# Router threshold and first expert pair: copies on VectorE, the p product's stores on GpSimd's queue and from other buffers, the first pair's columns gathered one 128 at a time

## The chip, the cores and the metric

One core of one Trainium2 chip. The metric is the device time of the kernel in microseconds (us). The kernel before took 1686.97 us, the median of 3 runs (1686.44 to 1687.9).

## The reference, cut to what matters

Two transformer blocks run one after the other on 512 tokens of width 1024, all in float32. The first block ends in an expert-choice mixture: 16 experts, and each takes its 64 best tokens.

```
logits = einsum('btd,de->bte', h, w_router)
affinity = softmax(logits, axis=-1)                       # 512 tokens x 16 experts
gate, idx = lax.top_k(swapaxes(affinity, 1, 2), 64)
xe = h[idx]                                               # 64 tokens of each expert
a = einsum('becd,edf->becf', xe, w_gate)
u = einsum('becd,edf->becf', xe, w_up)
ye = einsum('becf,efd->becd', silu(a) * u, w_down) * gate
out.at[idx].add(ye)                                       # back to the tokens
```

The second block needs, near its end, `p_2 @ w_ple_2` (512x256 by 256x1024). It depends on inputs alone.

## The kernel before

The order of the work on each engine is written by hand: an instruction goes into its engine's queue in the order of the source, and each engine works its queue from the front. SP issues the weight loads, ACT and GpSimd (POOL) a few other DMAs.

**Output projection and router (up to L1226).** `out_quarter` runs the last product of the first block's attention part in four quarters on PE. Beside it `half_T`, `half_mm`, `rms`, `logit` and `soft` compute the router's softmax, one 128-token tile `t` after the other. `rms(t)` adds two sums on VectorE (DVE), scales them there (L186), takes the power on POOL (L182), and issues the store of the tile's rows to `x1_d` in DRAM from ACT (L1114). `x1_d` is read again much later, by the indirect gathers (L1323) of pairs 1 to 7.

**The p product (L1156 to L1169).** `pw_tile(i)` computes one half of one token tile of `p_2 @ w_ple_2`: two matmuls on PE, a copy of the PSUM bank by ACT (L1166), and after the second half of a tile a store to `pw_d` in DRAM, issued by ACT (L1168). There are eight such halves. Tiles 0 and 3 are copied to `xe[:, 0]`, tile 1 to `xe[:, 1]`, tile 2 to a part of `pk`. They are spread over the router so that PE has work: halves 0 and 1 beside the softmax of the last tile, 2 to 5 beside the top-64 search, 6 and 7 beside the threshold's use. `pw_d` is read back near the end of the kernel.

**Top 64 (L1229 to L1258).** The affinities are transposed (L1220) to 64 rows of 128, and DVE takes the 64 largest of each row in eight rounds (L1236, L1238) into `tops`. Then four sorted lists per expert are merged: two of them are moved to other partitions (L1244 by DVE, L1245 by ACT), a first maximum is taken (L1246), and twelve small DVE instructions sort and merge down to the threshold `thr`. All of it lies in the buffers `affT` and `tops`, two of the four buffers of the pool `tp`; the others of the pool serve `xT`, then `Gu` and `Gs`.

**Slots (L1260 to L1294).** PE brings the threshold to all partitions (`rt`), DVE compares (L1263, L1264), PE counts (L1269 to L1273), and DVE builds one-hot matrices (`onehot`, L1287) of which token sits in which slot: `Gu[0]` for the first pair of experts, `Gs`, the same times the token's norm, and `Gu[1]`.

**Expert pairs (L1427 to L1513).** Two experts at a time, in eight pairs; each pair has three products: `pa_` (gate), `pu` (up), `py` (down). `pair_gemm` runs a product in four quarters; a quarter reads two weight tiles of 1 MB (`ew`), and right after a quarter's matmuls SP gets the loads that reuse those two buffers (`eload`). Loads for pair 0 are issued long before; further ones wait until a buffer comes free. For pair 0 the tokens' columns come from matmuls with `Gs`: `gather(k0, n)` writes `n` columns of 128 into one PSUM bank (8 PE instructions a column), and ACT copies each to `xe[:, 0, k]` (L1304). Quarter `q` needs columns 2q and 2q+1. Before, columns 0 to 3 are gathered ahead of quarter 0, columns 4 and 5 ahead of quarter 1, 6 and 7 ahead of quarter 2. The other pairs get their tokens by an indirect DMA on POOL's queue.

**Second block.** After the last pair the rest of the kernel runs mostly on PE.

Of the kernel before, what the change touches and what calls it, by code (L numbers as in the profile page):

```python
# [12 lines left out]
AF = mybir.ActivationFunctionType  # L13
# [5 lines left out]
NT = T // 128  # L19
# [44 lines left out]
def tile_two_blocks(ctx: ExitStack, tc: tile.TileContext, a, out):  # L64
    nc = tc.nc
    ACT, DVE, PE, POOL, SP = nc.scalar, nc.vector, nc.tensor, nc.gpsimd, nc.sync
# [33 lines left out]
    def bank(name="pb", shape=(512,), dt=F32):  # L100
        return cur["ps"].tile([128] + list(shape), dt, name=name, tag="b")
# [30 lines left out]
    for gi, g in enumerate(groups):  # L132
        r = 0
        for n in g:
            v, k = rows(n)
# [48 lines left out]
    def rstd(dst, src, n, eps):  # L184

        DVE.tensor_scalar(dst, src, 1.0 / n, eps, op0=OP.mult, op1=OP.add)  # L186
        power(dst)
# [130 lines left out]
    def run(gen):  # L318
        for _ in gen:
            pass  # L320
# [53 lines left out]
    p_ = bank()  # L374
# [667 lines left out]
    def xrow(t, s=slice(None)):  # L1042
        return xr[t // 2][:, t % 2, s]

    def half(n):
        return slice(n * 512, n * 512 + 512)

    def dcol(k):

        return slice(256 * (k // 2) + k % 2, 256 * (k // 2) + 256, 2)  # L1050

    ga2 = cp.tile([128, 8], F32, name="ga2")
    DVE.tensor_scalar(ga2, modd[:, 8:16], 1.0, None, op0=OP.add)
    DVE.tensor_mul(ga2, ga2, bmp[:, 16:24])
    sh2 = modd[:, 0:8]
# [16 lines left out]
    def s1(t):  # L1072
        return aff[:, t, 17:18]
# [4 lines left out]
    affT = tp.tile([128, 512], F32, name="affT", tag="t")  # L1078
    tops = tp.tile([128, 512], F32, name="tops", tag="t")
# [31 lines left out]
    def rms(t):  # L1111
        DVE.tensor_add(s1(t), sq1[:, t, 0:1], sq1[:, t, 1:2])
        rstd(s1(t), s1(t), D, 1e-6)
        ACT.dma_start(out=x1_d[t * 128:t * 128 + 128], in_=xrow(t))  # L1114

    pls, mxs = {}, {}
# [8 lines left out]
    def logit(t):  # L1125

        l = lg[:, t]
        DVE.tensor_add(l, l, pls[t])
        DVE.scalar_tensor_tensor(l, l, s1(t), rb, op0=OP.mult, op1=OP.add)
        mxs[t] = mx = small("mx", 2)  # L1130
        DVE.tensor_reduce(mx[:, 0:1], l, axis=mybir.AxisListType.X, op=OP.min)
        ACT.activation(l, l, AF.Exp, bias=mx[:, 0:1], scale=-1.0, accum_out=mx[:, 1:2])

    def soft(t):
        sm = mxs[t][:, 1:2]
        DVE.reciprocal(sm, sm)
        DVE.tensor_scalar(aff[:, t, :16], lg[:, t], sm, None, op0=OP.mult)


    pw_d = dp.tile([128, NT, D], F32, name="pw_d")  # L1140
    pw = {}
# [15 lines left out]
    def pw_tile(i):  # L1157
        t, n = i // 2, i % 2
        p_ = bank("pw")
        for k in range(2):  # L1160
            PE.matmul(p_, pw["p"][:, 1, k * 512 + t * 128:k * 512 + t * 128 + 128], pw["w"][:, k, half(n)],
                      start=(k == 0), stop=(k == 1))
            yield
        o = pw["p"][:, 0] if t == 2 else xe[:, t % 2].rearrange("p k c -> p (k c)") if t < 2 else \
            xe[:, 0].rearrange("p k c -> p (k c)")
        ACT.activation(o[:, half(n)], p_, AF.Copy)  # L1166
        if n:
            ACT.dma_start(out=pw_d[:, t], in_=o)  # L1168
        yield  # L1169


# [32 lines left out]
    xe = big("xe", [2, KT, 128])  # L1204
    half_mm(2, 1)
    half_T(NT - 1, 1)
    rms(2)
    logit(2)
    gpw = pw_tile(0)
    next(gpw)  # L1210
    soft(2)
    half_mm(NT - 1, 1)
    rms(NT - 1)
    logit(NT - 1)
    run(gpw)
    gpw = pw_tile(1)
    next(gpw)
# [24 lines left out]

    l0, l1, ls, lb = (affT[:, c:c + 64] for c in (129, 193, 257, 322))
    DVE.tensor_copy(ls[0:32], tops[32:64, 0:64])  # L1244
    ACT.activation(ls[64:96], tops[96:128, 0:64], AF.Copy)  # L1245
    DVE.tensor_tensor(l0[0:96], tops[0:96, 0:64], ls[0:96, ::-1], op=OP.max)  # L1246
    x_, y_, d = l0, l1, 32
    while d:
# [3 lines left out]
        x_, y_, d = y_, x_, d // 2  # L1252
# [3 lines left out]
    DVE.tensor_tensor(affT[:16, 0:65], affT[:16, 128:193], affT[:16, 321:386][:, ::-1], op=OP.min)  # L1256
    thr = cp.tile([16, 1], F32, name="thr")
    DVE.tensor_reduce(thr, affT[:16, 0:65], axis=mybir.AxisListType.X, op=OP.max)  # L1258

    rt = bank3("rt")  # L1260
    PE.transpose(rt[:, 0, 0:16], thr.to_broadcast([16, 128]), ident[:16, :16])
    th = rt[:, 0, None, 0:16].to_broadcast([128, NT, 16])
    DVE.tensor_tensor(ge[:, :, 0:16], aff[:, :, 0:16], th, op=OP.is_gt)  # L1263
    DVE.tensor_tensor(ge[:, :, 16:32], aff[:, :, 0:16], th, op=OP.is_equal)  # L1264
    gpw = pw_tile(6)
    next(gpw)

    cnt = rt[:, 1, 0:128].rearrange("p (t c) -> p t c", t=NT)
    PE.matmul(cnt, tri, ge, start=True, stop=False)  # L1269
# [2 lines left out]
    for t in range(NT):  # L1272
        PE.matmul(cnt[:, :, 16:32], ones, ge[:, t, None, 0:16].to_broadcast([128, NT, 16]), start=False,  # L1273
                  stop=(t == NT - 1))
# [17 lines left out]
    Gs = tmp("Gs", (NT, 128))  # L1292
    DVE.tensor_mul(Gs, Gu[0], aff[:, :, 17:18].to_broadcast([128, NT, 128]))
    onehot(1)  # L1294

    def gather(k0, n):

        p_ = bank("pg", (n, 128))
        for d in range(n):
            for t in range(NT):  # L1300
                PE.matmul(p_[:, d], xrow(t, dcol(k0 + d)), Gs[:, t], start=(t == 0), stop=(t == NT - 1))
        for d in range(n):
            k = k0 + d
            ACT.activation(xe[:, 0, k], p_[:, d], AF.Identity, bias=sh2[:, k:k + 1], scale=ga2[:, k:k + 1])  # L1304

    gt_ = cp.tile([128, 8], F32, name="gt_")
    sl = cp.tile([128, 8], F32, name="sl")
# [121 lines left out]
    for p in range(8):  # L1429
# [5 lines left out]
        pa_ = bank3("pa_")  # L1435
        side = []
        if p == 0:
            gather(0, 2)
            side = [lambda q=q: gather(2 * q, 2) for q in (1, 2, 3)]
        else:  # L1440
            side = [lambda: None] + [lambda t=t: combine(p - 1, t) for t in ((0,), (1,), (2, 3))]
        pair_gemm(pa_, i0, xlhs, side)
# [4 lines left out]
        side = [lambda: gates(p + 1) if p < 7 else None, lambda: gates(0) if not p else None]  # L1447
# [4 lines left out]
        for n in range(2):  # L1452
            p_ = bank("pg", (4, 128))
# [9 lines left out]
        side = []  # L1463
        if p < 7:
            slots(p + 1, 0)
            side = [lambda: None, lambda: slots(p + 1, 1)]
# [27 lines left out]
        for n in range(2):  # L1494
            for q, (k0, nk) in enumerate(lasts[n]):
# [8 lines left out]
                for k in range(k0, k0 + nk):  # L1504
                    for e in range(2):
                        PE.matmul(py[n][64 * e:64 * e + 64], hlhs(k, e), tiles[e][k - k0], start=(k == 0),  # L1506
                                  stop=(k == KT - 1), tile_position=(0, 64 * e))
# [480 lines left out]
```

## Time and profile before

| What | us |
|---|---|
| median of 3 runs | 1686.97 |
| profiled execution | 1687.58 |
| its span in the profile | 1685.8 |
| TensorE busy | 1624.6 (96% of the span) |
| VectorE busy | 924.6 (55%) |
| ScalarE busy | 568.6 (34%) |
| GpSimd busy | 58.1 (3%) |

The profiled execution is 0.61 us above the median, and 1.78 us of it lie outside the span. Times in the trace are counted from the start of the span. A matmul in float32 shows as two PE instructions; PE's matmuls overlap, so an instruction's duration is longer than the distance to the next.

### The profile page before, as it was taken

How to read it: one execution, taken by the hardware profiler on the slowest of the kernel's cores; microseconds unless marked ns; L12 is line 12 of the kernel's file. 1: busy time of each engine (PE TensorE's matmuls, PEld its weight loads, DVE VectorE, ACT ScalarE, POOL GpSimd, SP SyncE). 2: the span in 40 equal slices, each digit the busy share in tenths (PEclk: the TensorE clock that was granted, in tenths of full speed). 3: DMA queues.
4: the chain of work that ended last, by engine and by line, in shares of the span. 5: the costliest groups of instructions: out<-in, count | busy, mean ns of one | idle time of the engine just before them, and what ended most of it. 6: DMA issues, size and time to landing. Idle time of an engine off the chain costs nothing.

```text
span 1685.8 us, 20663 instructions
## 1 busy us (share of the span) xinstructions
PE 1624.6 (96%) x8266; PEld 1140.7 (68%) x8266; DVE 924.6 (55%) x1760; ACT 568.6 (34%) x1070; POOL 58.1 (3%) x69
## 2 busy tenths in 40 slices
PE   8999999999999996999999898999999999999997
PEld 5987787767888883433334333358898888877886
DVE  4667676565554342122321231168889999845555
ACT  5454544455323231110000001052436532354234
POOL 2000000000000000000000000010001000000000
PEclk9999999999999998999999999999999999999999
DMA  9232323111554595999999999963323233333341
GB/s 356 71 103 98 102 99 101 51 51 51 200 193 132 226 362 225 394 425 427 426 427 426 427 426 427 420 215 89 95 81 96 84 92 100 100 100 100 100 150 50
DMA packets 139396, 341.26 MB, mean 202 GB/s; under 512 B 6719, under 2 KB 91492, under 8 KB 115620
## 3 DMA queue, kind: packets, MB, share of 16 engines
q1 hardware_dynamic: 135504, 328.50, 52.0%
q0 software_dynamic: 2272, 6.58, 1.1%
q10 hardware_dynamic: 1524, 4.86, 0.8%
q8 instruction: 65, 1.06, 0.3%
q14 instruction: 31, 0.25, 0.0%
HBM read 333.62 MB, written 6.29 MB: 202 GB/s over the span
## 4 chain that ended last, share of the span: by engine, by line
PE 35%; DMA 11%; DVE 2%; issue 1%; ACT 1%; POOL 0%; POOLq 0%; SPq 0%; ACTq 0%; DVEq 0%
PE pb L297 9%; PE pb L298 9%; PE pb L299 9%; DMA ew<-w_exp_up 4%; DMA ew<-w_exp_down 4%; DMA ew<-w_exp_gate 3%; PE py L1358 1%; PE pv L299 1%; PE pv L297 1%; PE pv L298 1%; PE pa__6628 L1358 1%; PE pu L1358 1%; PE py L1506 1%; PE pb L1620 1%; DMA xe<-x_d,ix 1%
## 5 line engine op out<-in xcount | busy, mean ns | idle before, releaser
L256 DVE TENSOR_TENSOR wl<-wr,wh 128x512 fp32r<-128x512 f32 x340 | 229.5, 696 | 120.2 <-ACT wh L258 120.2
L258 ACT ACTIVATE wh<-wr 128x512 fp32r<-128x512 f32 x340 | 194.6, 621 | 111.3 <-PE pb L298 58.8
L1699 DVE SCALAR_TENSOR_TENSOR co<-cin,cols,co 128x512 f32<-128x512 f32 x240 | 191.4, 797 | 4.2
L297 PE MATMUL pb<-h2h,wh 128*128 128x512 f32 x432 | 170.7, 395 | 0.0
L298 PE MATMUL pb<-h2l,wh 128*128 128x512 f32 x432 | 168.3, 390 | 0.0
L299 PE MATMUL pb<-h2h,wl 128*128 128x512 f32 x432 | 168.3, 390 | 0.0
L297 PE MATMUL pb<-hxh,wh 128*128 128x512 f32 x320 | 130.4, 408 | 0.0
L1358 PE MATMUL pu<-ew,xe 128*64 128x512 f32 x512 | 116.3, 595 | 9.9 <-DMA ew<-w_exp_up 9.8
L298 PE MATMUL pb<-hxl,wh 128*128 128x512 f32 x320 | 125.2, 391 | 0.0
L299 PE MATMUL pb<-hxh,wl 128*128 128x512 f32 x320 | 125.1, 391 | 0.0
L1358 PE MATMUL py<-ew,hb 128*64 128x512 f32 x440 | 102.4, 596 | 2.7 <-DMA ew<-w_exp_down 2.7
L297 PEld LDWEIGHTS pb<-h2h,wh 128*128 128x128 f32 x432 | 81.1, 188 | 19.0 <-issue 2.4
L1358 PEld LDWEIGHTS pu<-ew,xe 128*64 128x64 f32 x512 | 38.7, 137 | 80.6 <-issue 60.9
L299 PEld LDWEIGHTS pb<-h2h,wl 128*128 128x128 f32 x432 | 81.1, 188 | 17.1
L298 PEld LDWEIGHTS pb<-h2l,wh 128*128 128x128 f32 x432 | 81.1, 188 | 16.9 <-issue 0.5
L1375 DVE TENSOR_TENSOR xr<-pg,xr 128x512 f32<-128x512 f32 x64 | 41.6, 686 | 69.2 <-PE pg L1374 67.9
L855 ACT ACTIVATE P<-P,m 128x512 f32<-128x512 f32 (+1 forms) x64 | 49.7, 777 | 85.8 <-DVE m L854 83.2
L1450 DVE TENSOR_TENSOR hb<-pu,hb 128x512 f32<-128x512 f32 x16 | 10.3, 686 | 122.8 <-PE pu L1358 63.7
L851 DVE CUSTOM_DVE_ANT_0 P<-s,cst,sink 128x512 f32<-128x512 f32 (+1 forms) x64 | 52.2, 815 | 46.3 <-PE s L848 45.9
L1358 PEld LDWEIGHTS py<-ew,hb 128*64 128x64 f32 x440 | 32.2, 137 | 61.7 <-issue 53.3
L299 PEld LDWEIGHTS pb<-hxh,wl 128*128 128x128 f32 x320 | 60.1, 188 | 13.6
L297 PEld LDWEIGHTS pb<-hxh,wh 128*128 128x128 f32 x320 | 60.2, 188 | 11.4 <-issue 2.3
(473 smaller groups left out, 3003.6 us busy)
## 6 DMA issues: line engine op xcount, KB each, us to landing
ew<-w_exp_gate SPq DMA_DIRECT2D x64, 1024.0 KB, 19.5
ew<-w_exp_up SPq DMA_DIRECT2D x64, 1024.0 KB, 19.7
wr<-w_in SPq DMA_DIRECT2D x58, 1024.0 KB, 5.9
ew<-w_exp_down SPq DMA_DIRECT2D x55, 1024.0 KB, 19.7
wr<-w_mod SPq DMA_DIRECT2D x16, 1024.0 KB, 5.1
wm<-w_mod SPq DMA_DIRECT2D x8, 1024.0 KB, 13.2
wr<-w_out SPq DMA_DIRECT2D x8, 1024.0 KB, 5.9
ew<-w_exp_down SPq DMA_DIRECT2D x16, 512.0 KB, 10.5
```

The costliest lines, as they stand in the source:

```text
L256: (lo_engine or DVE).tensor_tensor(lo[:, ks], raw[:, ks], hi[:, ks].bitcast(F32), op=OP.subtract)
L258: ACT.activation(hi[:, ks], raw[:, ks], AF.Copy)
L297: PE.matmul(ps, ah, bh, start=first, stop=False)
L298: PE.matmul(ps, ah, bl, start=False, stop=False)
L299: PE.matmul(ps, al, bh, start=False, stop=last)
L851: DVE.tensor_tensor_reduce(p_[:, :n], s2[:, self.s0:self.s0 + n], self.mask, 1.0, sink8[:, 4 * g + i:4 * g + i + 1], op0=OP.add, op1=OP.ma ...
L855: ACT.activation(p_[:, :n], p_[:, :n], AF.Exp, bias=m4[:, i:i + 1], scale=0.125, accum_out=sm[:, i:i + 1])
L1358: PE.matmul(ps[64 * e:64 * e + 64, n], lhs(k, e), tiles[e][kk][:, n * 512:n * 512 + 512], start=(k == 0), stop=(k == KT - 1), tile_positio ...
L1375: DVE.tensor_add(xrow(t, half(n)), p_, xrow(t, half(n)))
L1506: PE.matmul(py[n][64 * e:64 * e + 64], hlhs(k, e), tiles[e][k - k0], start=(k == 0), stop=(k == KT - 1), tile_position=(0, 64 * e))
L1620: PE.matmul(ps[m], w_[:, k, m * 128:m * 128 + 128], x_(k), start=(k == 0 and z == 0), stop=(k == KT - 1 and z == 2))
L1699: DVE.scalar_tensor_tensor(co[ct], cin[ct][:, k:k + 512], ctap(k, ct), co[ct], op0=OP.mult, op1=OP.add)
```

## The change

- The second list copy (L1245) moves from ACT to DVE.
- `pw_tile`: the stores to `pw_d` are issued by POOL. Tile 3 no longer goes to `xe[:, 0]`: its first half is copied to `affT`, its second to `tops`, and each half is stored by itself, so there are five stores in place of four.
- The first matmul of half 6 is issued ahead of the threshold's transposition, in place of behind the compares.
- `rms` of the last token tile is issued ahead of `soft(2)`; its store to `x1_d` is issued behind `logit` of that tile.
- `gather` takes a PSUM bank for each column, and ACT copies it before the next column's matmuls are issued. Columns 0, 1, 2 come ahead of quarter 0, then 3, 4, then 5, 6, then 7.

```diff
     def rms(t):
         DVE.tensor_add(s1(t), sq1[:, t, 0:1], sq1[:, t, 1:2])
         rstd(s1(t), s1(t), D, 1e-6)
+        if t < NT - 1:
+            x1_put(t)
+
+    def x1_put(t):
         ACT.dma_start(out=x1_d[t * 128:t * 128 + 128], in_=xrow(t))
...
-        o = pw["p"][:, 0] if t == 2 else xe[:, t % 2].rearrange("p k c -> p (k c)") if t < 2 else \
-            xe[:, 0].rearrange("p k c -> p (k c)")
-        ACT.activation(o[:, half(n)], p_, AF.Copy)
-        if n:
-            ACT.dma_start(out=pw_d[:, t], in_=o)
+        if t == 3:
+            o = tops if n else affT
+            ACT.activation(o, p_, AF.Copy)
+            POOL.dma_start(out=pw_d[:, t, half(n)], in_=o)
+        else:
+            o = pw["p"][:, 0] if t == 2 else xe[:, t].rearrange("p k c -> p (k c)")
+            ACT.activation(o[:, half(n)], p_, AF.Copy)
+            if n:
+                POOL.dma_start(out=pw_d[:, t], in_=o)
         yield
...
     next(gpw)
+    rms(NT - 1)
     soft(2)
     half_mm(NT - 1, 1)
-    rms(NT - 1)
     logit(NT - 1)
+    x1_put(NT - 1)
     run(gpw)
...
     DVE.tensor_copy(ls[0:32], tops[32:64, 0:64])
-    ACT.activation(ls[64:96], tops[96:128, 0:64], AF.Copy)
+    DVE.tensor_copy(ls[64:96], tops[96:128, 0:64])
...
     DVE.tensor_reduce(thr, affT[:16, 0:65], axis=mybir.AxisListType.X, op=OP.max)
+    gpw = pw_tile(6)
+    next(gpw)
 
     rt = bank3("rt")
     PE.transpose(rt[:, 0, 0:16], thr.to_broadcast([16, 128]), ident[:16, :16])
     th = rt[:, 0, None, 0:16].to_broadcast([128, NT, 16])
     DVE.tensor_tensor(ge[:, :, 0:16], aff[:, :, 0:16], th, op=OP.is_gt)
     DVE.tensor_tensor(ge[:, :, 16:32], aff[:, :, 0:16], th, op=OP.is_equal)
-    gpw = pw_tile(6)
-    next(gpw)
...
-    def gather(k0, n):
-
-        p_ = bank("pg", (n, 128))
-        for d in range(n):
+    def gather(*ks):
+
+        for k in ks:
+            p_ = bank("pg", (128,))
             for t in range(NT):
-                PE.matmul(p_[:, d], xrow(t, dcol(k0 + d)), Gs[:, t], start=(t == 0), stop=(t == NT - 1))
-        for d in range(n):
-            k = k0 + d
-            ACT.activation(xe[:, 0, k], p_[:, d], AF.Identity, bias=sh2[:, k:k + 1], scale=ga2[:, k:k + 1])
+                PE.matmul(p_, xrow(t, dcol(k)), Gs[:, t], start=(t == 0), stop=(t == NT - 1))
+            ACT.activation(xe[:, 0, k], p_, AF.Identity, bias=sh2[:, k:k + 1], scale=ga2[:, k:k + 1])
...
         if p == 0:
-            gather(0, 2)
-            side = [lambda q=q: gather(2 * q, 2) for q in (1, 2, 3)]
+            side = [lambda k=k: gather(*k) for k in ((0, 1, 2), (3, 4), (5, 6), (7,))]
```

## Rows read from the trace of the kernel before

**Rows 1.** The page's first two parts: busy time of each engine, then three lines of the span in 40 equal slices of 42.1 us (tenths: PE busy, granted TensorE clock, DMA engines busy).

```profile
PE 1624.6 (96%) x8266; PEld 1140.7 (68%) x8266; DVE 924.6 (55%) x1760; ACT 568.6 (34%) x1070; POOL 58.1 (3%) x69
PE   8999999999999996999999898999999999999997
...
PEclk9999999999999998999999999999999999999999
DMA  9232323111554595999999999963323233333341
```

**Rows 2.** Windows, the expert pairs' stretch. Columns: window, its length, busy us (and number of instructions) of PE, PEld, DVE, ACT, POOL, then granted clock, DMA share, GB/s.

```profile
693.00:720.00 27.00, 26.68 (x130) 10.09 (x128) 6.66 (x15) 3.02 (x5) 0.00 (x0) 1.00 1.00 412
900.00:1096.00 196.00, 177.08 (x770) 72.82 (x768) 42.21 (x87) 15.19 (x23) 1.87 (x2) 1.00 1.01 425
```

**Rows 3.** Windows of 2 us in the stretch of the threshold and the first pair; the same columns.

```profile
644.00:646.00 2.00, 0.00 (x0) 0.00 (x0) 1.59 (x11) 0.20 (x1) 0.00 (x0) 0.72 1.02 414
...
648.00:650.00 2.00, 2.00 (x11) 0.88 (x10) 0.01 (x1) 0.00 (x0) 0.00 (x0) 0.50 0.02 8
...
652.00:654.00 2.00, 2.00 (x10) 1.19 (x9) 0.59 (x1) 0.87 (x2) 0.00 (x0) 1.00 0.00 0
...
660.00:662.00 2.00, 0.00 (x0) 0.00 (x0) 0.00 (x0) 0.00 (x0) 0.00 (x0) 0.99 0.97 408
...
668.00:670.00 2.00, 2.00 (x9) 0.56 (x6) 0.00 (x0) 0.00 (x0) 0.00 (x0) 0.80 0.00 0
...
694.00:696.00 2.00, 2.00 (x12) 0.72 (x10) 0.00 (x0) 1.15 (x1) 0.00 (x0) 1.00 0.94 303
```

**Rows 4.** Timeline, the last token tile's softmax. Columns: start us, duration us, engine, line, operation, out and in with shapes, count, and in brackets the idle time before it and what ended it.

```profile
631.73 0.24 DVE L1129 SCALAR_TENSOR_TENSOR lg<-lg,aff,rb 128x16 f32<-128x16 f32 x1 [0.39 <-POOL aff L182]
...
633.21 0.30 PE L1220 MATMUL pt<-cst,aff 128*128 128x128 f32 x1 [0.28 <-DVE aff L1137]
```

**Rows 5.** Timeline, from the end of the top-64 search to the threshold; the same columns.

```profile
637.21 4.03 PE L1161 MATMUL pw<-wpl,pk 128*128 128x512 f32 x9
...
639.23 0.18 DVE L1244 COPY affT<-tops 32x64 f32<-32x64 f32 x1
...
642.46 1.08 ACT L1166 ACTIVATE pk<-pw 128x512 f32<-128x512 f32 x2 [4.02 <-DMA x_d<-xr]
...
643.95 0.25 ACT L1245 ACTIVATE affT<-tops 32x64 f32<-32x64 f32 x1 [0.40 <-ACT pk L1166]
644.24 0.22 DVE L1246 TENSOR_TENSOR affT<-tops,affT 96x64 f32<-96x64 f32 x1 [4.82 <-ACT affT L1245]
...
647.18 0.28 PE L1261 MATMUL rt<-cst,thr 16*128 16x16 f32 x1 [5.94 <-DVE thr L1258]
```

**Rows 6.** Timeline, from the threshold to the gather; the same columns.

```profile
647.40 2.08 PE L1161 MATMUL pw<-wpl,pk 128*128 128x512 f32 x2
...
647.64 0.21 DVE L1264 TENSOR_TENSOR tri__5069<-aff,rt 128x64 bf16<-128x64 f32 x1
...
649.27 0.31 PE L1269 MATMUL rt<-tri__5069 128*128 128x128 bf16 x1
...
649.76 3.78 PE L1161 MATMUL pw<-wpl,pk 128*128 128x512 f32 x6
649.99 0.29 DVE L1275 TENSOR_TENSOR tops<-tri__5069,rt 128x128 f32<-128x128 bf16 x1 [2.13 <-PE rt L1273]
...
651.30 0.69 DVE L1293 TENSOR_TENSOR Gs<-Gu,aff 128x512 f32<-128x512 f32 x1
...
653.38 3.92 PE L1301 MATMUL pg<-Gs,xr 128*128 128x128 f32 x32
```

**Rows 7.** Timeline, pair 0's gate product from the gather on; the same columns.

```profile
654.21 0.33 ACTq L1168 DMA_DIRECT2D pw_d<-xe  x1
663.24 1.50 ACT L1304 ACTIVATE xe<-pg,modd,ga 128x128 f32<-128x128 f32 x4 [9.06 <-DMA pw_d<-xe]
...
663.75 6.13 PE L1358 MATMUL pa__5646<-ew,xe 128*64 128x512 f32 x16 [6.44 <-ACT xe L1304]
...
669.81 2.15 PE L1301 MATMUL pg<-Gs,xr 128*128 128x128 f32 x16
...
671.89 3.65 PE L1358 MATMUL pa__5646<-ew,xe 128*64 128x512 f32 x16
...
684.58 1.07 PE L1314 MATMUL pg<-aff,Gu 128*128 128x18 f32 x8
```

**Rows 8.** Timeline of SP's own DMA queue: weight loads issued after the p product's last matmuls, after quarter 0 of the gate product, and after quarter 1 of the up product.

```profile
653.62 0.80 SPq L1003 DMA_DIRECT2D ew<-w_exp_down  x2
...
669.91 0.81 SPq L1003 DMA_DIRECT2D ew<-w_exp_down  x2
...
693.83 0.80 SPq L1003 DMA_DIRECT2D ew<-w_exp_gate  x2
```

**Rows 9.** DMAs issued by POOL elsewhere in the kernel: one issue in the timeline of POOL, the window behind it (columns as in Rows 2), and two lines of the DMA issues (KB each, us from issue to landing).

```profile
1120.42 1.01 POOL L1641 DMA_DIRECT2D wsb<-a_ws  x1 [0.32 <-issue]
...
1122.00:1124.00 2.00, 2.00 (x15) 1.78 (x14) 1.40 (x3) 2.00 (x4) 1.07 (x3) 1.00 0.87 213
...
wsb<-a_ws POOLq DMA_DIRECT2D x1, 512.0 KB, 4.5
...
xe<-x_d,ix POOLq DMA_INDIRECT x7, 8.5
```

## The prediction

> **What bounds the kernel now.** I read the page first [rows 1]. PE is busy 96% of the span, so idle PE is the first thing to look for; the deepest gap is in the sixteenth slice, 632 to 674, where the granted clock also falls short and where the DMA engines are at five tenths between slices at nine. That is the threshold and the start of expert pair 0. Next the windows of the pairs [rows 2]: from 693 to 1096 the DMA engines have a share of 1.00 and move 412, then 425 GB/s, while PE has 19 us to spare after 900. The pairs are bound by the weight stream, and what decides when they end is when that stream starts to run without a break.
>
> Then the 2 us windows ahead of it [rows 3]. The DMA engines are full up to 646, empty at 648 and 652, full around 660, empty at 668, and lightly short for the last time at 694. They are empty because SP waits for buffers that PE has not yet read: it issues two loads at 653.62, two after quarter 0 at 669.91, and the last two that come into an unfilled stream at 693.83, on the release by quarter 1 of the up product [rows 8]. From there 425 GB/s and a fixed number of bytes set the end. So the end moves by as much as PE's way to 693.83 moves, and that way I follow backwards in the timelines.
>
> On it stand two stalls. ACT has a store to `pw_d` to issue and is held until 642.46, 4.02 us, by an earlier store of `x1_d`; behind it in ACT's queue stands the list copy of 643.95, and DVE, done with its own copy at 639.41, waits 4.82 us for that [rows 5]. Later ACT waits 9.06 us, from 654 to 663.24, until the store of tile 3 has read `xe[:, 0]`, before it can put the gathered columns there; PE, done with the gather at 657.3, waits 6.44 us [rows 7]. Both idle times also drop the granted clock to its lower level, 0.50 of 2.4 GHz, that is 1.2 GHz: it is 0.72 in the window at 644, 0.50 at 648, and 0.80 in the window at 668 on its way back [rows 3].
>
> **The change part by part.** *rms moved.* DVE's L1129 had waited 0.39 us for the last tile's power on POOL; issued ahead of `soft(2)` it is done in time. The transposition had waited only 0.28 us for the chain [rows 4], since PE itself is busy before: I take 0.3. The store of `x1_d`, behind `logit(3)`, stands ahead of ACT's first p copies; its issue takes a third of a microsecond, as 654.21 does [rows 7], while ACT would wait for PE, so nothing; were it held as ACT was before 642.46, by 4 us, the p copies behind it would be late, PE would wait for banks, and `rt`, behind the p matmuls in PE's queue, would lose up to 4 of the gain below. That end goes into the range.
>
> *List copy on DVE.* It adds one DVE copy like the first (0.18, with the step to the next 0.22) and takes out 4.82 of idle time [rows 5]: 4.6 us. With rms, the transposition `rt` moves from 647.18 to 642.3. PE's earlier p matmuls end at 641.24, now 640.9 [rows 5]. The first half of half 6, two instructions of 0.43 (nine take 4.03 with the last one's tail [rows 5]), ends at 641.8. PE is free half a microsecond before `rt`.
>
> *Half 6's first matmul moved.* Before, its two instructions stood between the compares (end 647.85) and the counts (649.27), at the lower clock [rows 6]. Compares' end to DVE's L1275 took 2.14 us. Without them and at the higher clock the count matmuls take between 0.35 and 0.69 us (649.27 to 649.96, halved or not); with 0.5 and 0.1 for the hand-over it is 0.6: 1.5 us less. L1275 then starts at 643.6.
>
> *Clock.* The six p instructions left (649.76 to the gather at 653.38, 3.4 us from the end of the counts [rows 6]) take 6 x 0.43 = 2.6 at the higher clock: 0.8 us less. The gather starts at 646.15; `Gs`, 6.4 us earlier than 651.99, is ready at 645.6 and in front. Sum up to here 0.3 + 4.6 + 1.5 + 0.8 = 7.2.
>
> *Stores from POOL and from other buffers.* The wait for tile 3's store goes. What is late next is tile 0's store out of `xe[:, 0]`: its copy ends near 634.7, POOL's issue costs 1.0, and the landing took 4.5 for a load with an idle stream and 8.5 for the gathers behind a full one [rows 9]. It lands at 640 to 645; the first gathered column wants the buffer at 647.2. So nothing, with 2 us in hand. No row shows a store issued by POOL. ACT's store of 654.21 took 9 behind two loads [rows 7], which still fits. Tile 3's two stores hold `affT` and `tops`, and of the pool's next tenants `Gu[1]` is wanted by no one before the up product at 668; if DVE waits for it, nothing else is queued on DVE before that. GpSimd has nothing else queued before the gather for pair 1, 16 us after its last store. SP's two loads of 653.62 need the `pk` buffer, thus tile 2's store, and the last p matmul; they come some 6 us earlier.
>
> *Gather.* Three columns in place of four stand ahead of quarter 0. Four took 3.92 for 32 instructions [rows 6], three take 2.94; ACT's copies at 0.37 each (four in 1.50 [rows 7]) lie beside the next column, as do the copies of 3, 5 and 7 beside the quarter's first half. Quarter 0 starts at 649.1 in place of 663.75: gather to quarter was 10.37 and is 2.94, 7.4 us less.
>
> *Clock again.* Quarter 0 took 6.06 (663.75 to 669.81) and quarter 1, of the same 16 instructions, 3.6 [rows 7]. With no idle PE ahead of it I give quarter 0 the second: 2.4 less. It ends at 652.75, 17.0 earlier than before.
>
> *Column 7* returns ahead of quarter 3: two columns cost 2.08 (669.81 to 671.89 [rows 7]), one 1.0. The gate product thus ends at 668.6 in place of 684.58 [rows 7].
>
> Sum: 7.2 + 7.4 + 2.4 - 1.0 = 16.0 us. From the up product on the order is as before, so the release of 693.83 comes at 677.8, and the stream and all behind it move by 16.0. The profiled execution of 1687.58 becomes 1671.6; by the median, 0.61 lower, 1671.0, my forecast.
>
> **Rivals.** *A: part is given back.* If the clock falls although PE idles only half a microsecond before `rt` and half before the counts (the two drops of [rows 3] stand in idle times of 5.94 and 6.44 us [rows 5, 7]), gather and quarter 0 run at the lower level for 2.4 to 5 us. Or the stream still has a backlog at 677.8, and gains only the emptiness taken out: two holes of about 8 us, around 648 to 654 and 662 to 670 [rows 3], of which I leave 2 to 3, an estimate. Or ACT is held at the moved store. These give 11 to 14 us: 1673 to 1676.
>
> *B: GpSimd can't issue beside a busy DVE.* DVE works from 633.5 until the one-hots end near 646.3. If tile 0's store only starts then, it lands at 655 (8.5 of [rows 9]); column 0 goes out then, PE stands still from 648, the clock falls and quarter 0 ends near 662.5: 7.3 less 1.0, so 6.3 us gained, 1680.7. Against it: POOL's loads of 1120 queued up beside a DVE busy 1.40 of 2 us, and 213 GB/s flowed in that window [rows 9]. The Trainium skill speaks for it: "SBUF — State Buffer", section "SBUF: two separate sides", warns that a DMA issued by GpSimd stalls while DVE runs an operation that holds the port pair the two share, such as a float32 copy from SBUF to SBUF, and that issue from ACT or SP escapes this. By that rule a store waits out DVE's copies; no run here shows a store by GpSimd yet.
>
> *C: a new wait takes the old one's place.* If `Gu[0]` gets the buffer of `tops`, it waits for tile 3's second store: copied at 646.7, landed 1.0 + 8.5 later, at 656.3; with `onehot` and `Gs` of 0.69 each the gather starts at 657.7, quarter 0 at 660.7 at the lower clock, and ends at 666.8: 3.0 less 1.0, 2 us gained, 1685, within 0.2%. The change would then not do what it says. Against it: two other buffers of that pool have stood empty since `xT`'s last use.
>
> *D: slower.* SP's queue is in order, and its next loads need `pk`, now read by a store on POOL's queue. While that store is late, no weight load is issued at all. Up to 693.83 ten loads are due after 647 (at 2.47 us for 1.05 MB at 425 GB/s, 24.7 us); the stream catches up if they begin before about 669, and each us after that is one lost: a landing at 673 makes 1691. That is 31 us after the copy; the nearest rows are 4.5 and 9.
>
> **How the numbers follow.** The forecast's own case 0.74 (1669.5 to 1672.8: 0.5 for the counts, 0.5 for hand-overs, the releases' spacing), A 0.12, B 0.06, C 0.04, D 0.02, unnamed 0.02. About 0.2%, 3.4 us, is what a measurement of this kernel can tell from no change. Faster are the forecast's case, A and B and half of the unnamed, 0.93; same C and the other half, 0.05; slower D, 0.02. The range from 1669.3 to 1676.5 holds nearly all of the first and of A, 0.8 or a little more.
>
> **What would show it.** DVE's L1246 behind the second copy with no wait; `rt` near 642.3; granted clock 1.00 in all windows from 640 to 672; ACT's first gathered copy waiting for PE, not for a store; quarter 0 from 649.1 to 652.8; loads issued near 652.8 and 677.8; the first quarter of the second pair's gate product 16 us earlier. The prediction is wrong if a `pw_d` store stands as the releaser of a gathered copy or of `Gu[0]`, if the clock shows 0.50 there, or if PE's 16 us are there at 678 and not at 1096.

## The result and the profile after

The kernel after took 1671.01 us, the median of 4 runs (1670.37 to 1673.86), against 1687.43 for the kernel before on the same chip (4 runs, 1686.44 to 1689.5): a ratio of 0.9904, 95% interval 0.9887 to 0.9922. The forecast was 1671.0 (taken from the 1686.97 us measured before it). The profiled execution took 1671.03 us, with a span of 1669.3.

The page after, the lines that answer to [rows 1]:

```profile
PE 1620.3 (97%) x8266; PEld 1138.5 (68%) x8266; DVE 924.3 (55%) x1761; ACT 569.0 (34%) x1069; POOL 60.6 (4%) x74
...
PE   8999999999999999999999898999999999999998
...
PEclk9999999999999999999999999999999999999999
DMA  9232333111554499999999999943332323323241
```

In the sixteenth slice the DMA line's five has become a nine and so has PE's six, and the granted clock is nine in all slices: the gap that the prediction started from is gone.

Before two traces are compared, their executions must be put on one scale. One matmul of the output projection (L299), well ahead of everything that the change touches, starts at 603.94 before and at 603.07 after. So 0.87 us of what the later times differ has nothing to do with the change, and "net" below means with that taken out, for each run by the same matmul.

The timeline after, from the p product's first store to pair 0's gate product, all engines (start, duration, engine, line, operation, count, idle time before and what ended it):

```profile
634.29 0.59 POOL L1176 DMA_DIRECT2D pw_d<-xe  x1 [4.37 <-ACT xe L1174]
...
637.73 0.54 POOL L1176 DMA_DIRECT2D pw_d<-xe  x1 [2.84 <-DMA x_d<-xr]
...
638.27 0.19 DVE L1254 COPY affT<-tops 32x64 f32<-32x64 f32 x1
638.49 0.22 DVE L1255 TENSOR_TENSOR affT<-tops,affT 96x64 f32<-96x64 f32 x1
...
641.45 0.22 PE L1272 MATMUL rt<-cst,thr 16*128 16x16 f32 x1 [0.52 <-DVE thr L1267]
...
642.38 2.82 PE L1165 MATMUL pw<-wpl,pk 128*128 128x512 f32 x6
642.58 0.29 DVE L1284 TENSOR_TENSOR tops<-tri__5069,rt 128x128 f32<-128x128 bf16 x1 [0.52 <-PE rt L1282]
...
644.52 0.55 POOL L1171 DMA_DIRECT2D pw_d<-affT  x1 [2.88 <-ACT affT L1170]
...
645.03 3.05 PE L1310 MATMUL pg<-Gs,xr 128*128 128x128 f32 x24
...
646.22 0.46 ACT L1311 ACTIVATE xe<-pg,modd,ga 128x128 f32<-128x128 f32 x1 [0.34 <-PE pg L1310]
...
647.98 0.69 DVE L1296 TENSOR_TENSOR Gu<-cst,post 128x512 f32<-128x512 f32 x1 [3.40 <-DMA pw_d<-affT]
648.02 3.65 PE L1365 MATMUL pa__5647<-ew,xe 128*64 128x512 f32 x16
...
667.66 1.07 PE L1321 MATMUL pg<-aff,Gu 128*128 128x18 f32 x8
...
676.91 0.80 SPq L1003 DMA_DIRECT2D ew<-w_exp_gate  x2
```

Read it against [rows 5 to 8]. The first merge step, L1255, follows the second copy with no wait, where it had waited 4.82 us. `rt` has 0.52 us of idle PE ahead of it and not 5.94. The first gathered copy waits for PE, not 9.06 us for a store, and quarter 0 starts right behind the gather and takes 3.65, not 6.13. The pair of loads that had been issued at 693.83 is issued at 676.91: 16.92 us earlier, 16.05 net.

Windows after, in the columns of [rows 2, 3]:

```profile
644.00:646.00 2.00, 2.00 (x12) 1.35 (x10) 0.58 (x1) 0.71 (x2) 0.55 (x1) 1.00 1.03 420
...
648.00:650.00 2.00, 2.00 (x11) 0.78 (x12) 0.68 (x1) 0.46 (x1) 0.00 (x0) 1.00 0.67 184
...
668.00:670.00 2.00, 2.00 (x15) 1.11 (x15) 0.45 (x4) 0.89 (x2) 0.79 (x1) 1.00 0.70 209
...
678.00:680.00 2.00, 2.00 (x12) 0.72 (x10) 0.00 (x0) 1.15 (x1) 0.00 (x0) 1.00 0.86 315
...
900.00:1080.00 180.00, 161.41 (x696) 65.52 (x694) 36.98 (x75) 12.85 (x20) 1.87 (x2) 1.00 1.01 425
```

The granted clock is 1.00 in every window from 636 to 696. The weight stream still has dents (0.67, 0.70, 0.86 of its share) but no window near zero any more, and behind 680 it runs at 425 GB/s as before.

Further on the clock did fall, in a place that the change does not touch. At the start of the second block (its first matmuls, `hT`) PE waits 2.46 us for VectorE in either trace. The lines of that place, before and after, as windows and as the group of the `hT` matmuls (instructions, then busy us, mean ns of one, idle us before them; 2.9 is the 2.46 and a later 0.44):

```profile
1116.00:1120.00 4.00, 2.93 (x23) 2.74 (x24) 3.50 (x16) 2.81 (x9) 1.99 (x3) 1.00 0.02 6
L1578 PE MATMUL hT<-dg,xf 128*128 128x128 f32 x41 | 5.1, 280 | 2.9 <-DVE dg L1562 2.9
...
1100.00:1104.00 4.00, 4.00 (x23) 4.00 (x23) 2.66 (x11) 1.96 (x5) 2.00 (x3) 0.58 0.03 6
L1584 PE MATMUL hT<-dg,xf 128*128 128x128 f32 x44 | 6.8, 330 | 2.5 <-DVE dg L1568 2.5
```

At the last pair's final matmuls the change is 16.4 us ahead net; behind this place it is 15.5.

### The profile page after: what moved, and what is told of

Same layout as the page of the kernel before. It is cut to its first block, busy times and chain, and to the rows that moved or that the text cites. A ratio compares the mean times of both kernels' runs of the same rounds, so it can differ in the third digit from the quotient of the medians.

```text
span 1669.3 us, 20670 instructions
## 1 busy us (share of the span) xinstructions
PE 1620.3 (97%) x8266; PEld 1138.5 (68%) x8266; DVE 924.3 (55%) x1761; ACT 569.0 (34%) x1069; POOL 60.6 (4%) x74
## 3 DMA queue, kind: packets, MB, share of 16 engines
q10 hardware_dynamic: 948, 2.76, 0.4%
## 4 chain that ended last, share of the span: by engine, by line
PE 43%; DMA 13%; DVE 2%; issue 1%; ACT 1%; POOL 0%; POOLq 0%; ACTq 0%; SPq 0%; DVEq 0%
PE pb L297 9%; PE pb L298 9%; PE pb L299 9%; DMA ew<-w_exp_up 5%; DMA ew<-w_exp_gate 5%; PE py L1365 3%; DMA ew<-w_exp_down 2%; PE pu L1365 2%; DMA xe<-x_d,ix 1%; PE pv L299 1%; PE pv L297 1%; PE pv L298 1%; PE pa__6149 L1365 1%; PE pa__6391 L1365 1%; PE pa__5907 L1365 1%
## 5 line engine op out<-in xcount | busy, mean ns | idle before, releaser
L299 PE MATMUL pb<-h2h,wl 128*128 128x512 f32 x432 | 168.3, 390 | 0.0
L299 PE MATMUL pb<-hxh,wl 128*128 128x512 f32 x320 | 125.1, 391 | 0.0
L299 PEld LDWEIGHTS pb<-h2h,wl 128*128 128x128 f32 x432 | 81.1, 188 | 17.1
L299 PEld LDWEIGHTS pb<-hxh,wl 128*128 128x128 f32 x320 | 60.1, 188 | 13.6
L297 PEld LDWEIGHTS pb<-hxh,wh 128*128 128x128 f32 x320 | 60.2, 188 | 11.4 <-issue 2.3
## 6 DMA issues: line engine op xcount, KB each, us to landing
wm<-w_mod SPq DMA_DIRECT2D x8, 1024.0 KB, 12.4
```

What stands on the lines that cost most here:

```text
L297: PE.matmul(ps, ah, bh, start=first, stop=False)
L299: PE.matmul(ps, al, bh, start=False, stop=last)
```

## The experiments

Each run gives two readings. The first is its time. The second is where two landmarks stand in its trace, net, against the same matmuls before: pair 0's up product (the matmul at 688 before) and the second block (the matmul at 1300). The landmarks tell tenths of a microsecond apart where the times can't, but each is read from one execution, the profiled one. Differences of medians also hold what an execution happened to gain elsewhere: the change's profiled one had its 0.87 us in hand before anything changed. In the table ScalarE, VectorE and PE are the engines ACT, DVE and TensorE. (In e11, which reorders the up product, the first one is taken in the down product behind it.)

| Kernel | Median us | Ratio to before, 95% | Up product, net us | Second block, net us |
|---|---|---|---|---|
| the change as a whole | 1671.01 | 0.9904 (0.9887 to 0.9922) | -16.0 | -15.5 |
| e1, change, list copy on ScalarE | 1676.34 | 0.9935 (0.9918 to 0.9952) | -12.2 | -9.9 |
| e2, change, stores by ScalarE | 1676.14 | 0.9933 (0.9916 to 0.9949) | -12.9 | -10.6 |
| e3, change, tile 3 in `xe` | 1677.5 | 0.9945 (0.9928 to 0.9961) | -10.9 | -9.8 |
| e4, change, old grouping of the gather | 1672.24 | 0.9916 (0.9899 to 0.9932) | -16.5 | -16.5 |
| e5, before, list copy on VectorE | 1680.63 | 0.9953 (0.9936 to 0.997) | -3.6 | -3.0 |
| e6, before, tile 3 in other buffers | 1679.41 | 0.9956 (0.9939 to 0.9972) | -9.2 | -9.7 |
| e7, before, PE's wait filled | 1685.77 | 0.9989 (0.9979 to 0.9998) | -2.8 | -2.7 |
| e8, change, half 6 behind the compares | 1672.52 | 0.9913 (0.9896 to 0.9929) | -15.6 | -14.4 |
| e9, change, `rms` in its old place | 1671.86 | 0.9902 (0.9886 to 0.9919) | -15.7 | -15.9 |
| e10, change, PE 4.4 us later | 1676.97 | 0.9937 (0.992 to 0.9953) | -11.8 | -11.2 |
| e11, change, gate product 0 moved | 1672.44 | 0.991 (0.9893 to 0.9927) | -15.9 | -15.0 |
| e12, as e1, PE's wait filled | 1674.5 | 0.9918 (0.9901 to 0.9934) | -13.6 | -10.9 |

My theory was the prediction's sum. The rival that stayed after the result was that one edit does nearly all of it and the others are cover.

**e1: the list copy undone.**

```diff
-    DVE.tensor_copy(ls[64:96], tops[96:128, 0:64])
+    ACT.activation(ls[64:96], tops[96:128, 0:64], AF.Copy)
```

> The changed kernel with one edit undone: the second list copy is ACT's again. Theory: the copy was late because it stood in ACT's queue behind a store whose issue was held; with the stores on POOL nothing holds ACT, and the copy comes right behind the last p copy in front of it, which ends at 640.7 in the changed kernel's trace. DVE's L1255 then starts near 641.0 in place of 638.5, so 2.5 us slower than the changed kernel, 1673.5. Rival: moving the copy is what took out 4.6 us, whoever issues the stores; then about 4.6 slower, 1675.6, as the prediction's sum has it.

By the medians it cost 5.3 us, above both; by the up product 3.8, between them. The timeline of e1:

```profile
641.28 0.60 ACT L1174 ACTIVATE pk<-pw 128x512 f32<-128x512 f32 x1 [1.12 <-PE pw L1165]
641.90 0.25 ACT L1254 ACTIVATE affT<-tops 32x64 f32<-32x64 f32 x1
...
642.19 0.22 DVE L1255 TENSOR_TENSOR affT<-tops,affT 96x64 f32<-96x64 f32 x1 [2.76 <-ACT affT L1254]
...
645.14 0.23 PE L1272 MATMUL rt<-cst,thr 16*128 16x16 f32 x1 [3.04 <-DVE thr L1267]
...
646.26 4.01 PE L1165 MATMUL pw<-wpl,pk 128*128 128x512 f32 x6
```

and its windows (columns as above):

```profile
644.00:646.00 2.00, 0.42 (x4) 0.42 (x5) 1.30 (x8) 0.00 (x0) 0.00 (x0) 0.81 1.01 412
646.00:648.00 2.00, 2.00 (x10) 1.07 (x9) 1.41 (x4) 0.00 (x0) 0.00 (x0) 0.50 0.59 242
```

With no store to hold it, ACT's queue still delivers the copy 2.76 us late, since two copies of `pk` that wait for PE stand ahead of it. Then PE is idle for 3.04 us, the granted clock falls to 0.50, and the six p matmuls take 4.01 and not 2.82. Of the 3.8 us, 2.5 are lateness (`rt`, net) and, if the clock is the cause of the rest, 1.3 are the clock. e12 tests that.

**e12: the same with PE kept busy.** Three matmuls whose results nobody reads stand in that wait.

```diff
     rt = bank3("rt")
+    for i in range(3):
+        PE.matmul(rt[:, 0], ident, xrow(0, half(0)), start=True, stop=True)
```

> The changed kernel with the list copy back on ScalarE (which alone gave 1676.3 us) and three more 128x512 matmuls, whose results nobody reads, in the 3.0 us that TensorE then idles ahead of the threshold's transpose: six passes at 0.443 us, 2.7 us. VectorE's chain is as late as in that run. Theory: of the 3.8 us by which that run's releases came later, 2.5 are the late list and 1.3 the clock that fell in the idle time; with the wait filled the six matmuls of the p product take 2.8 us again and not 4.0, the releases come 1.3 us earlier than there, and the time is about 1675.0 us. Rival: the idle time and the clock have nothing to do with each other here; the six matmuls take 4.0 us again and the time stays at 1676.3 us.

The timeline of e12:

```profile
642.04 2.74 PE L1273 MATMUL rt<-xr,cst 128*128 128x512 f32 x6
645.24 0.22 PE L1274 MATMUL rt<-cst,thr 16*128 16x16 f32 x1 [0.47 <-DVE thr L1267]
...
646.18 2.82 PE L1165 MATMUL pw<-wpl,pk 128*128 128x512 f32 x6
```

and its windows:

```profile
644.00:646.00 2.00, 1.09 (x5) 0.31 (x4) 1.40 (x9) 0.00 (x0) 0.00 (x0) 1.00 1.02 416
646.00:648.00 2.00, 2.00 (x13) 1.04 (x13) 1.52 (x4) 0.60 (x1) 0.00 (x0) 1.00 0.69 283
```

VectorE is as late as in e1 (`rt` at 645.24), but the clock stays at 1.00, the six matmuls take 2.82 again, and the up product comes 1.4 us earlier than in e1. Useless work on PE won back what the idle time had cost. The median, 1.8 us lower, has the same sign; the two intervals overlap.

**e2: the stores undone.**

```diff
-                POOL.dma_start(out=pw_d[:, t], in_=o)
+                ACT.dma_start(out=pw_d[:, t], in_=o)
```

(and the same for tile 3's two stores)

> The changed kernel with the five stores of the p product issued by ACT in place of POOL; buffers, copies and order as changed. Theory: what removes the 9 us is the other buffers, so the gathered columns still don't wait for a store; ACT is held again at an issue for some us until an earlier transfer lands, which delays p copies, PE for want of PSUM banks, and the threshold's transposition behind them by 0 to 4 us: 1671 to 1675, best guess 1673. Rival: POOL's queue is what lets the stores land in time; then the store of tile 0 or a held ACT costs 7 us or more, 1678 and up.

By the medians it cost 5.1 us, by the up product 3.1. The timeline of e2:

```profile
642.09 1.09 ACT L1174 ACTIVATE pk<-pw 128x512 f32<-128x512 f32 x2 [4.03 <-DMA x_d<-xr]
...
642.74 1.13 PE L1165 MATMUL pw<-wpl,pk 128*128 128x512 f32 x2 [1.88 <-ACT pk L1174]
...
644.92 4.24 PE L1165 MATMUL pw<-wpl,pk 128*128 128x512 f32 x6
```

ACT is held for 4.03 us, as before (4.02, [rows 5]). The trace's records fit one reason: the held store is to announce its landing on the same semaphore (the counter that tells of a transfer's end) as the `x1_d` store of 631.83, whose last part landed at 641.36, and it is issued 0.36 us after that. In the kernel before, e5 and e6 the same pair of stores shares a semaphore, and the gap is 0.35 to 0.36 us. GpSimd's five stores have semaphores of their own. No list copy stands behind it now, but the p copies do; PE wants their PSUM bank for half 6, waits 1.88 us, and again the six matmuls run at the lower level, 4.24. What the prediction feared of the moved `x1_d` store, p copies late and PE without a bank, happens as soon as a `pw_d` store is ACT's to issue.

**e3: tile 3 back in `xe[:, 0]`**, its store still by GpSimd.

```diff
-        if t == 3:
-            o = tops if n else affT
...
+        o = pw["p"][:, 0] if t == 2 else xe[:, t % 2 if t < 2 else 0].rearrange("p k c -> p (k c)")
```

> The changed kernel with tile 3 of the p product copied to xe[:, 0] again and stored from there whole, by POOL. The first gathered copy then waits for this store. Theory: the store was 9 us late in the kernel before because two weight loads had been queued in front of it; now the loads are issued only when the store of pk lands (647.2), the store is issued at 646.0 ahead of them and lands near 648.4, as the one from tops did at 648.5. Gather's copies start 2.2 us later and PE idles under 2 us, so the clock holds: about 2 us slower than the changed kernel, 1673. Rival: the wait of 9 us and the lower clock come back whole, since the stream of weights is served first; then 8 to 10 us slower, 1680.

By the medians it cost 6.5 us, between the two; by the up product 5.2. The timeline of e3:

```profile
647.11 0.53 POOL L1171 DMA_DIRECT2D pw_d<-xe  x1 [4.65 <-ACT xe L1169]
648.07 0.89 SPq L1003 DMA_DIRECT2D ew<-w_exp_down  x2
...
650.88 0.81 ACT L1306 ACTIVATE xe<-pg,modd,ga 128x128 f32<-128x128 f32 x2 [4.18 <-DMA pw_d<-xe]
...
653.40 4.27 PE L1360 MATMUL pa__5646<-ew,xe 128*64 128x512 f32 x16
```

The wait for the store is back but lasts 4.18 and not 9.06 us: here the store is issued 0.96 us ahead of SP's two loads and lands 3.7 us later, while in [rows 7, 8] it was issued 0.6 us behind them and landed after 8.9. The queue differs too, GpSimd's here and ScalarE's there; e2 and e6 tell the two apart (last section). PE idles for 3.43 us ahead of the third column, and the clock, which the theory had hold, falls to 0.50 in the window from 652.

**e4: the old grouping of the gather**, with everything else as changed: two columns to a bank, columns 0 to 3 ahead of quarter 0.

```diff
-            side = [lambda k=k: gather(*k) for k in ((0, 1, 2), (3, 4), (5, 6), (7,))]
+            gather(0, 2)
+            side = [lambda q=q: gather(2 * q, 2) for q in (1, 2, 3)]
```

> The changed kernel with the gather as it was: two columns in a bank, columns 0 to 3 ahead of quarter 0, then 4 and 5, then 6 and 7. Theory: quarters 0, 1 and 2 end 1.0 us later each, the gate product ends where it did, since as many columns stand ahead of its end; the release that decides (quarter 1 of the up product) does not move: no change, 1671.0 to 1671.4. Rival: the finer gather is worth what it gives at quarter 0 and more, because each of the early releases feeds the weight stream: 1 to 2 us slower.

The times can't be told apart. By the trace the new grouping is 0.4 us worse at the up product, not better.

**e5 and e6: the two large edits alone, on the kernel before.**

```diff
-    ACT.activation(ls[64:96], tops[96:128, 0:64], AF.Copy)
+    DVE.tensor_copy(ls[64:96], tops[96:128, 0:64])
```

> The kernel before with one part of the change alone: the second list copy on DVE. Theory: DVE goes on at 639.4, the threshold comes 4.6 us earlier; the p half between compares and counts then runs at the higher clock, and so do the six behind the counts, since PE has idled for 1.5 us only: the gather starts 6 us earlier, tile 3's store is issued 6 us earlier, and the wait for it, its length unchanged, moves with it: 6 us faster than before, 1681. Rival 1: 4.6 and nothing behind it, 1682.4. Rival 2: the store's landing is set by the loads ahead of it, which wait for the landing of pk's store and do not move: 2 us or less.

For e6 tile 3's two halves go to `affT` and `tops` with a store each, issued by ACT.

> The kernel before with one part alone: tile 3 of the p product goes to affT and tops, each half stored by itself, by ACT as before; list copy, order and gather as before. Theory: the first gathered copy no longer waits; PE goes from the gather at 657.3 straight into quarter 0, which starts near 657.5 at the higher clock and ends at 661.1 in place of 669.8: 8.7 us faster, 1678.5. Rival: the wait moves, to a one-hot that needs the buffer of affT or tops, or to ACT, which now issues two stores ahead of the gathered copies: 0 to 4 us.

The timelines, first of e5 with a window, then of e6:

```profile
642.74 0.22 PE L1261 MATMUL rt<-cst,thr 16*128 16x16 f32 x1 [1.36 <-DVE thr L1258]
644.19 1.23 PE L1161 MATMUL pw<-wpl,pk 128*128 128x512 f32 x2 [1.22 <-ACT pk L1166]
...
645.71 4.20 PE L1161 MATMUL pw<-wpl,pk 128*128 128x512 f32 x6
...
646.00:648.00 2.00, 2.00 (x3) 0.87 (x3) 1.90 (x5) 0.19 (x1) 0.00 (x0) 0.50 0.82 336
...
659.48 1.51 ACT L1304 ACTIVATE xe<-pg,modd,ga 128x128 f32<-128x128 f32 x4 [8.93 <-DMA pw_d<-xe]
```

```profile
646.98 0.28 PE L1265 MATMUL rt<-cst,thr 16*128 16x16 f32 x1 [5.91 <-DVE thr L1262]
...
653.03 3.92 PE L1305 MATMUL pg<-Gs,xr 128*128 128x128 f32 x32
656.89 3.65 PE L1362 MATMUL pa__5647<-ew,xe 128*64 128x512 f32 x16
```

In e5 `rt` comes 4.6 us earlier net, the prediction's term to the tenth, but PE then waits another 1.22 us for the copies that ACT still holds back. The theory had the clock hold; it fell to 0.50, and the six p matmuls behind took 4.20 us. So 3.6 us reach the up product, and the store's 8.93 us stand untouched. In e6 the first wait stands (5.91) and the second is gone, with quarter 0 at 3.65: 9.2 us. The four runs of e5 spread widely (1677.16 to 1684.9), and the profiled one is the slowest. So the 3.6 us are those of the slowest execution; the median is 6.3 us below that of the kernel before, near the theory's 6, and what the list copy brings alone is known no better than 2 to 10 us.

**e7: is it the idle time that slows quarter 0?** Six matmuls in PE's wait for the gathered columns, on the kernel before.

```diff
+            fill = bank3("fill")
+            for i in range(6):
+                PE.matmul(fill[:, i % 2], ident, xrow(0, half(0)), start=True, stop=True)
```

> The kernel before with six matmuls of 512 columns (12 PE instructions, 5.2 us) added on PE behind the first four gathered columns, into a PSUM bank that nothing reads; they fill most of the 6.44 us that PE waits there. No other edit. Theory: quarter 0 starts when it did, 663.75, but at the higher clock, and takes 3.6 in place of 6.06: 2.4 us faster than before, 1684.6, with granted clock 1.00 from 658 to 672. Rival: quarter 0 was slow for another reason (its first weight tiles, the copies' pace), or the fill delays it: no change or slower.

The timeline of e7:

```profile
657.76 5.32 PE L1442 MATMUL fill<-xr,cst 128*128 128x512 f32 x12
664.29 3.65 PE L1358 MATMUL pa__5646<-ew,xe 128*64 128x512 f32 x16 [1.22 <-ACT xe L1304]
```

Quarter 0 takes 3.65 and not 6.13 us though it waits for the same store. The trace gives 2.8 us at the up product, the median 1.1 with an interval that holds 2.8.

**e8 and e9: the two small edits undone**: half 6's first matmul behind the compares again, and `rms(3)` with its store ahead of the logit.

> The changed kernel with the first matmul of half 6 back behind the compares. Theory: PE idles 1.3 us ahead of the threshold's transposition, too little to lose the clock, and its two instructions stand between compares and counts again, now 0.43 each: counts 0.6 later and the gather 0.9 later: 0.9 us slower, 1671.9. Rival: the clock drops there, and the 1.5 and 0.8 of the prediction come back with the lower level for the gather on top: 3 to 5 us slower.

> The changed kernel with the last tile's rms and store put back behind its half product, ahead of the logit (the order of the kernel before). Theory: the softmax of the last tile starts some 0.3 us later and the whole chain behind it with it, so the last release into the unfilled weight stream comes 0.3 us later and the time is 1671.3 us. Rival: the softmax waits on something else than the engine order here, or the store, which now comes earlier on its queue, helps: no shift of the gather at all (0.0 us), 1671.0 us.

Their times are those of the change within the measurement. By the landmark half 6's place is worth 0.4 us and `rms` 0.3.

**e10 and e11: does the end follow the release?** In e10 five matmuls of pure delay stand ahead of the gather.

> The changed kernel with five more 128x512 matmuls, whose results nobody reads, on TensorE just ahead of pair 0's gather: ten passes at 0.443 us (5.3 us for twelve in the run with TensorE's wait filled), 4.4 us of pure delay at the full clock. Theory: the end follows TensorE's way to the last weight release one for one, so the last release moves by 4.4 us and the end too: 1675.4 us. Rival: between the last release and the end there is slack in the stream or in TensorE's later waits, and the end moves by under 3 us: 1672 to 1674 us.

In e11 pair 0's gate product is issued behind the up product's last quarter.

```diff
-        side = [lambda: gates(p + 1) if p < 7 else None, lambda: gates(0) if not p else None]
+        side = [lambda: gates(p + 1) if p < 7 else None]
         pair_gemm(pu, i0 + 8, xlhs, side)
+        if not p:
+            gates(0)
```

> The changed kernel with pair 0's gate product (8 matmuls, 0.99 us, ahead of quarter 1 of the up product) put behind that product's last quarter: its result is read only when pair 0's y is scaled. Theory: the last release into the unfilled stream (676.9 us) comes 1.0 us earlier, and the end with it: 1670.0 us, less still if the 0.3 us that TensorE waits for the first hidden half is filled. Rival: the weight stream behind the pair sets the end by itself from here on, or what is won in front is waited for in a later pair: 1671.0 us, with the release still 1.0 us earlier.

e10 moved the up product by 4.2 us and the second block by 4.3: one for one, by the theory. (Its median is 6.0 us above the change's; of the 5.3 between the two profiled executions 1.0 lies ahead of anything changed.) e11 fell on the rival's side. The release of e11 and its windows:

```profile
676.43 0.81 SPq L1003 DMA_DIRECT2D ew<-w_exp_gate  x2
```

```profile
668.00:670.00 2.00, 2.00 (x14) 1.31 (x14) 0.45 (x4) 1.08 (x2) 0.13 (x1) 1.00 0.45 119
678.00:680.00 2.00, 2.00 (x12) 0.67 (x10) 0.00 (x0) 0.47 (x1) 0.00 (x0) 1.00 1.02 418
```

Its release is 1.15 us earlier net, and the dent at 678 is filled (1.02 against 0.86). But that dent was only 0.14 of 2 us deep, so 0.3 us was all that filling it could give back, and the one at 668 is deeper in the same windows (0.45 against 0.70). No gain came of it. Its median of 1672.44 can't be told from that of the change.

## Why the prediction was right

**The number.** That the median met the forecast to 0.01 us is luck. Its four runs span 3.5 us, the profiled one had 0.87 us in hand ahead of all that was changed, and it lost as much again to the clock at the start of the second block. What is not luck is that the way to the release came out step by step.

**The bound.** Right. With all behind pair 0 unchanged, 16.05 us at the release are 16.4 at the last pair and 15.5 at the second block, and e10 gave 4.3 for 4.2. e11 narrows the sentence that the end follows the last release. As I read it, the end follows the emptiness that PE's way leaves in the stream: the whole way moved takes the stream along, and one late release alone can return no more than the dent behind it.

**The steps.** Net of 0.87, the trace has `rt` at 642.3 (forecast 642.3), the product with the counts at 643.5 (643.6), the gather at 645.9 (646.15), quarter 0 at 648.9 (649.1), the gate product's end at 668.5 (668.6), the release at 677.8 (677.8), and the profiled execution would be 1671.9 (1671.6). Each landmark is right within 0.3 us.

**The shares.** The sum was right; the division by edits was not, and no single-edit run could have told the total. The list copy was put at 4.6; alone it brought 3.6 in the one execution that was traced, the slowest of four, and its undoing cost 3.8, of which 1.4 was the clock (e12). Moving half 6 was put at 1.5 and was worth 0.4: the sum had counted it against rows taken at the lower clock. The stores were costed as if the wait for tile 3's store were all they removed. They also take ACT's held issue out (e2: 3.1 us at the up product), which the sum had booked under the list copy. Tile 3's buffers were the largest part, 9.2 alone, and 5.2 when undone. The undoings at the up product add up to 3.8 + 3.1 + 5.2 + 0.4 + 0.3 - 0.4 = 12.4, not 16.0, since most stalls had two edits against them: the store that no longer holds ACT and the copy that no longer stands behind it; other buffers and a store issued earlier.

**The gather's grouping.** Put at nothing (0.98 less ahead of quarter 0, 1.0 more later); measured 0.4 against it.

**The rivals.** A, part is given back: 0.6 us is, but not in the way that A names. The clock held through the threshold and pair 0, and the pairs gave nothing back; 0.9 us went at the start of the second block, where the clock fell in this execution. B fell: GpSimd issued its five stores in 0.53 to 0.59 us each, where the prediction had put 1.0. Three were issued beside a working VectorE, and the one at 637.73, across VectorE's copy at 638.06, took 0.54; the one at 644.52, with VectorE idle from 644.57 on, took 0.55, and so did the last, at 646.19, with VectorE idle throughout. Each started 0.31 to 0.45 us behind the end of the copy that it stores, the last the soonest. By the Trainium skill ("SBUF — State Buffer", section "SBUF: two separate sides") such a copy could have held an issue. The trace leaves at most the 0.06 us by which the five differ in length and 0.14 by which they differ in starting. C: `Gu[0]` waited for nothing; `Gu[1]` did wait 3.40 us for tile 3's store, and nobody was waiting for it, as foreseen. D: the `pk` store landed at 647.21, SP's next loads went out right behind it at 647.34, and the stream's dent there (0.67) is far from the point at which it would decide.

**What stays open.** Between the up product and the second block the change loses 0.6 us, e1, e2 and e12 lose 2.3 to 2.7, e3, e8 and e11 about 1, and e4, e6 and e9 none. Two things make this up. The first is the clock ahead of the second block: PE idles there for 2.46 us in all 14 traces, and in eight of them (the change, e1, e2, e5, e8, e10, e11, e12) the clock fell to 0.50 behind it and 0.7 to 1.2 us were lost; in the other six it stayed at 1.00 and nothing was. Why it fell in some was not tried, and with one trace of each kernel it isn't known whether it is the kernel or the single execution. The second is 1.3 to 1.5 us in e1, e2, e3 and e12. PE pays them in the fifth and sixth pair (900 to 1000), where it waits for weights, but the stream lost them earlier: by the trace's records of landings its loads come, from 760 to the last pair, 10.7 us (e1), 11.4 (e2), 9.4 (e3) and 12.1 (e12) earlier than before, net, where the release came 12.2, 12.9, 10.9 and 13.6 earlier; in the change both are 16.0 to 16.4. What held loads up there, between 700 and 755, was not tried. The traces of e1, e2, e5 and e12 are each of the slowest of four runs. So the column of the up product is the better measure of an edit, and the times of e1 and e2 overstate what the two edits are worth by some 2 us.

## What to carry to other kernels

When a stretch feeds a saturated stream, follow the engine's way to the last release and cost every edit on that way; what it takes out there comes back at the end nearly whole. Look behind each held instruction for everything queued on that engine: two edits against the same stall are not worth the sum of what each brings alone. And price an idle TensorE at more than its length, since the work behind it may run at half the clock; the length of one wait did not tell here whether it would.

## What the runs showed of the hardware

- Around the threshold, idle PE of 3.04 us (e1), 3.43 (e3) and 1.88 (e2), and of 1.36 and 1.22 with one short matmul between (e5), was followed by a granted clock of 0.50 to 0.59 in a 2 us window; after idle times of 1.37 (e8), 1.22 (e7) and 0.52 (after) it stayed at 1.00. The same 2.46 us ahead of the second block were followed by 0.50 in eight traces and by 1.00 in six. At 0.50, the lower level of 1.2 GHz, six p matmuls took 4.0 to 4.2 us in place of 2.82. Matmuls on data that nobody reads held the clock as well as useful ones (e7, e12).
- A 512 KB store on ScalarE's queue, issued 0.6 us behind two 1 MB loads on SP's queue, landed 8.9 us later, 0.2 us behind the second load; on GpSimd's queue, issued 0.96 us ahead of them, it landed after 3.7 (e3). On ScalarE's queue alone, by the trace's records of landings, tile 3's first 256 KB, issued 1.6 (e2) and 1.1 us (e6) ahead of the two loads, landed after 2.0 us; its second 256 KB, issued 0.6 us behind them, after 7.8 and 8.0. So on one queue the order against the loads alone made such a difference; a store by GpSimd behind the loads was not tried.
